# Subtracting two sets of low parts on POOL instead of VectorE in an encoder kernel

## The chip, the cores and the metric

The kernel runs on one core of one Trainium2 chip. The metric is the device time of one execution in microseconds (us); lower is better. The profiled times below come from one execution recorded by the hardware profiler. PE is the TensorE matrix engine, VectorE (DVE) does elementwise work, ACT is ScalarE, POOL is GpSimd, SP issues most DMAs.

## The reference, cut to what matters

One encoder layer with shared weights is applied to two groups of rows, a prompt of 256 and a sample of 1024, each row 1024 wide. The parts that matter here are the input projection and the expert layer:

```python
h = _rmsnorm(x, norm_mix[l])
(q_h, f_fw, f_bw, i_h, g_h, c_q, c_kv, k_pe, gl_h, gl_a) = jnp.split(h @ w_in[l], split_points, axis=-1)
y_h = _hgrn2_branch(...) @ w_br_h[l]
y_a = _mla_branch(...) @ w_br_a[l]
merged = jax.nn.sigmoid(gl_h) * y_h + jax.nn.sigmoid(gl_a) * y_a
x = x + merged @ w_out[l]
x = x + _peer(_rmsnorm(x, norm_ffn[l]), ...)

# _peer, for a block of 128 rows: 8 heads, 16 experts of 16384 for each
eidx, g = ...            # top 16 by product keys, softmax over their scores
u = jnp.take(u_tab, eidx, axis=0)
ve = jnp.take(v_tab, eidx, axis=0)
act = jax.nn.gelu(jnp.einsum('td,thkd->thk', zt, u), approximate=False) * g
return jnp.einsum('thk,thkd->td', act, ve)
```

All data are fp32.

## The kernel before

A product in fp32 precision is made from fp32r parts. `split` (L119 to L125) turns a tile into a high part, a cast on ACT (`nc.scalar.copy`, L123), and a low part, source minus high part, on VectorE (L124) or on an engine given as `eng`. `mm` then issues three matmuls: high by high (L140), high weight by low data (L141), low weight by high data (L142). With `whole` set, nothing is split and one plain fp32 matmul is issued (L138).

Two of the places that split weights are named by the change:

- The sample projection. `project` walks over 42 blocks of 128 columns of the input weights. `block` calls `load_w`: SP loads a `wraw` tile of 128x1024, ACT casts it to `wh`, and the low part becomes `wl`. Each block is multiplied with both halves of the 1024 sample rows, 48 matmuls a block. The prompt's projection runs the same code with `whole`, so it has no low part. `load_w` is also called for other weights (`wq`, `wo`, `wbh`, `wba`, `wuq`, `wk`, `wv`).
- The dense expert stage. 512 of the sample rows multiply with the whole expert tables. `first(b)`, for each of 128 blocks of 128 experts, loads `uraw` (128x1024) through `load_split`, splits it into `uh` and `ul`, multiplies it with the rows `zt` in 24 matmuls, applies gelu on ACT, multiplies by the gates (`ge`) on VectorE and splits the result into `ah` and `al`. `second(g)`, for each group of 4 blocks and each half of the 1024 output columns, loads and splits four `v` tiles (`vh`, `vl`, 128x512), issues 48 matmuls, and adds the results from PSUM into `acc` on VectorE (L1096).

The other rows, six groups of 128, go through gathered experts. POOL issues an indirect DMA for each of the 128 expert slots into a ring of 7 buffers of 128x1024. `u_steps` forms a dot product of each gathered `ug` with the row tile `zs` on VectorE (L938, L940). Then the `v` rows are gathered: `v_steps` weights and sums them on PE (L969, L976), while for two of the groups `v_slots` does it on VectorE, into `vacc` (L994, L996). These gathers run beside the sample projection, the attention and the dense expert stage until shortly before the end.

All queues are in order. The order in which instructions of independent parts are put on each engine's queue is set before the run by the framework's planner, which simulates a timeline with costs of its own; parts of the gathered path have higher priority there.

Of the kernel before, what the change touches and what calls it, by code (L numbers as in the profile page):

```python
# [24 lines left out]
P = 128  # L25
D = 1024
KD = D // P
# [23 lines left out]
def encoder(ctx, tc, I, O, dbg=None):  # L51
    nc = tc.nc
# [66 lines left out]
    def split(pool, src, shape, name, bufs=None, eng=None):  # L119
        kw = {} if bufs is None else {"bufs": bufs}  # L120
        hi = pool.tile(shape, F32R, name=name + "h", tag=name + "h", **kw)
        lo = pool.tile(shape, F32R, name=name + "l", tag=name + "l", **kw)
        nc.scalar.copy(hi, src)  # L123
        (eng or nc.vector).tensor_tensor(lo, src, hi.bitcast(F32), op=OP.subtract)  # L124
        return hi, lo  # L125

    def load_w(src, nk, cols, pool, whole=False, tag="w", bufs=3, nb=1, sp=None):
        raw = pool.tile([P, nk, cols], F32, name="wraw", tag=tag + "raw", bufs=bufs if tag == "w" else 1)  # L130
        cut = (lambda x: x.rearrange("p (b k) j -> p b k j", b=nb)) if nb > 1 else lambda x: x
        nc.sync.dma_start(cut(raw), src)
        x = (raw,) if whole else split(sp or pool, raw, [P, nk, cols], tag, bufs=2 if tag == "w" else 1)
        return [cut(a) for a in x]

    def mm(out, w, x, start, stop):
# [17 lines left out]
    def put(dst, src):  # L154

        if len(dst) == 1:
            nc.scalar.copy(dst[0], src)
        else:
            nc.scalar.copy(dst[0], src)
            nc.vector.tensor_tensor(dst[1], src, dst[0].bitcast(F32), op=OP.subtract)  # L160
# [43 lines left out]
    def project(s0, S, ap, wpool, bank, np_, whole):  # L204


        seg = min(S, 512)
        nseg = S // seg
        cps = seg // P
        H = parts(ap, [P, KD, S], "h", whole)  # L210
        ns = 256 if whole else 128
        for t0 in range(0, S, ns):
            xt = np_.tile([P, KD, ns], F32, name="xt", tag="xt", bufs=256 // ns)
            nc.sync.dma_start(xt, I["xT"][:, :, s0 + t0:s0 + t0 + ns])
            r = norm_T(np_, [xt[:, k] for k in range(KD)], KD, ns, "nA", bank, whole)
            for k in range(KD):
                hf = H[0][:, k, t0:t0 + ns] if whole else np_.tile([P, ns], F32, name="hf", tag="hf", bufs=3)
                nc.vector.scalar_tensor_tensor(out=hf, in0=xt[:, k], scalar=gains[:, G_MIX + k:G_MIX + k + 1],
                                               in1=r, op0=OP.mult, op1=OP.mult)
                if not whole:  # L220
                    put([a[:, k, t0:t0 + ns] for a in H], hf)
        yield

        def stage():
            return ap.tile([P, seg], F32, name="gt", tag="gt", bufs=3)

        def block(b, sink):
            w = load_w(I["wi"][b], KD, P, wpool, whole)
            for g in range(nseg):
                pm = bank()  # L230
                proj(pm[:, :seg], w, H, KD, g * seg, seg)
                sink(slice(s0 + g * seg, s0 + (g + 1) * seg), pm[:, :seg])

        def s_plain(dst, func=None):
            def f(ts_, pm):
                gt = stage()
                if func is None:
                    nc.scalar.copy(gt, pm)
                else:
                    nc.scalar.activation(out=gt, in_=pm, func=func)  # L240
                nc.scalar.dma_start(dst[:, ts_], gt)
            return f

        def s_silu(dst):
            def f(ts_, pm):
                gt = stage()
                nc.scalar.activation(out=gt, in_=pm, func=AF.Sigmoid)
                nc.vector.tensor_tensor(gt, pm, gt, op=OP.mult)
                nc.sync.dma_start(dst[:, ts_], gt)
            return f  # L250

        def s_forget(dst, c):
            def f(ts_, pm):
                gt = stage()
                nc.scalar.activation(out=gt, in_=pm, func=AF.Sigmoid)
                nc.scalar.activation(out=gt, in_=gt, func=AF.Identity, scale=omlb[:, c:c + 1], bias=lb[:, c:c + 1])
                nc.scalar.dma_start(dst[:, ts_], gt)
            return f

        def s_rows(dst):  # L260
            def f(ts_, pm):
                vT = stage()
                nc.scalar.copy(vT, pm)
                pt = bank()
                for c in range(cps):
                    nc.tensor.transpose(pt[:, c * P:(c + 1) * P], vT[:, c * P:(c + 1) * P], ident)
                gt = stage()
                nc.scalar.copy(gt, pt[:, :seg])
                nc.scalar.dma_start(dst[ts_].rearrange("(c p) j -> p c j", p=P), gt.rearrange("p (c j) -> p c j", j=P))
            return f  # L270

        for h in range(NH):
            block(B_FF + h, s_forget(fgd[1, h], h))
            block(B_FB + h, s_forget(fgd[0, h], NH + h))
            block(B_Q + h, s_silu(qhd[h]))
            block(B_I + h, s_rows(vhd[h]))
            block(B_G + h, s_silu(ghd[h]))
            yield
        for b in range(2):
            block(B_CKV + b, s_plain(lat[b]))  # L280
        block(B_PE, s_plain(lat[2]))
        for b in range(3):
            block(B_CQ + b, s_plain(lat[3 + b]))
        yield
        for b in range(8):
            block(B_GLH + b, s_plain(gated[b], AF.Sigmoid))
            block(B_GLA + b, s_plain(gated[8 + b], AF.Sigmoid))
        yield
# [766 lines left out]
            if t + 4 == TC:  # L1055
                nc.scalar.dma_start(gd[n * (P // TC) + c], gs[n, c].rearrange("p h t -> p (h t)"))

    def load_split(pool, src, shape, name, bufs):
        raw = pool.tile(shape, F32, name=name + "raw", tag=name + "raw", bufs=2)
        nc.sync.dma_start(raw, src)  # L1060
        return split(pool, raw, shape, name, bufs)

    def dense(routes, zt, acc, dp, up, bankS, bankV):

        nt = len(routes)
        nch = ND // TC
        held = {}
        a_of = {}

        def first(b):  # L1070
            u = load_split(up, I["uT"][b], [P, KD, P], "u", 2)
            if b % HB == 0:
                held["g"] = dp.tile([P, nch, HB, TC], F32, name="g", tag="g", bufs=2)
                nc.scalar.dma_start(held["g"].rearrange("p c h t -> p c (h t)"),
                                    gd[:, :, b * TC:(b + HB) * TC].rearrange("c p x -> p c x"))
            pm = bankS()
            for k in range(KD):
                mm(pm, [x[:, k] for x in u], [x[:, k] for x in zt], k == 0, k == KD - 1)
            ge = dp.tile([P, ND], F32, name="ge", tag="ge", bufs=2)
            nc.scalar.activation(out=ge, in_=pm, func=AF.Gelu)  # L1080
            gev = ge.rearrange("p (c t) -> p c t", t=TC)
            nc.vector.tensor_tensor(gev, gev, held["g"][:, :, b % HB], op=OP.mult)
            a_of[b] = (dp.tile([P, ND], F32R, name="ah", tag="ah", bufs=GE + 1),
                       dp.tile([P, ND], F32R, name="al", tag="al", bufs=GE + 1))
            put(a_of[b], ge)

        def second(g):
            for n in range(2):
                ns = slice(n * 512, (n + 1) * 512)
                vs = [load_split(dp, I["peer_v"][b * P:(b + 1) * P, ns], [P, 512], "v", 2 * GE)  # L1090
                      for b in range(g * GE, (g + 1) * GE)]
                for t in range(nt):
                    pm = bankV()
                    for i in range(GE):
                        mm(pm, [x[:, t * P:(t + 1) * P] for x in a_of[g * GE + i]], vs[i], i == 0, i == GE - 1)
                    nc.vector.tensor_tensor(acc[:, t, ns], pm, acc[:, t, ns], op=OP.add)  # L1096

        for t, r in enumerate(routes):
            nc.sync.dma_start(acc[:, t], x2d[r["tt"]:r["tt"] + P])
        first(0)  # L1100
        for g in range(P // GE):
            for b in range(g * GE + 1, (g + 1) * GE + 1):
                if b < P:
                    first(b)
            second(g)
        gfin = final_gain()
        for t, r in enumerate(routes):
            finish(acc[:, t], ring("sq"), r["tt"], gfin)
# [128 lines left out]
    up = ctx.enter_context(tc.tile_pool(name="DU", bufs=1, side="left"))  # L1237
# [78 lines left out]
```

## Time and profile before

| | |
|---|---|
| median of 3 runs | 4287.37 us (4286.51 to 4300.59) |
| profiled execution | 4300.6 us, span of the core 4298.8 us |
| busy PE / VectorE / ACT / POOL | 3802.2 / 3234.1 / 1559.9 / 1818.6 us |
| moved by DMA | 1263.92 MB, 294 GB/s on average |
| mean granted TensorE clock | 0.941 of full speed |

Busy times are sums over the whole span; an engine with a low share can still be full in one stage. A POOL instruction is mostly the issue of a gather, and its span in the profile is rough.

### The profile page before, as it was taken

The page shows a single profiled execution, that of the slowest core. Times are in us where ns is not written, and L with a number is a line of the kernel's source. Part 1 is how long each engine was busy: PE and PEld are TensorE (multiplying, and loading weights), DVE is VectorE, ACT ScalarE, POOL GpSimd, SP SyncE. Part 2 cuts the span into 40 slices and gives each one's busy share as a digit, 9 for nine tenths or more (in the row PEclk, how much of TensorE's full clock was granted, in tenths as well). Part 3 has the DMA queues.
Part 4 walks back from the last instruction along what each step waited for, and adds up shares of the span by engine and source line. Part 5 has one row for each costly group of instructions (what it writes and reads, how often), then busy time and mean ns, then how long its engine had stood idle before and what let it go on. Part 6 is the DMA issues. An engine that isn't in the chain of part 4 may idle for free.

```text
span 4298.8 us, 55005 instructions
## 1 busy us (share of the span) xinstructions
PE 3802.2 (88%) x18206; PEld 2734.5 (64%) x18206; DVE 3234.1 (75%) x8002; ACT 1559.9 (36%) x2600; POOL 1818.6 (42%) x1565
## 2 busy tenths in 40 slices
PE   6998999997777988877988489999999999899998
PEld 5777777775434753345644155677777877777786
DVE  4637988567988773986679985567668999999954
ACT  5555455454233214431201187522222222222232
POOL 0000644334444343774545512344446556666500
PEclk9999999998888999888999688999999999999999
DMA  5455899889999987998988847899999999999941
GB/s 160 123 183 152 324 344 343 315 305 319 318 311 313 323 312 272 328 339 326 334 293 285 292 181 292 325 322 339 334 333 356 339 358 362 365 364 346 326 140 64
DMA packets 508318, 1263.92 MB, mean 294 GB/s; under 512 B 49920, under 2 KB 203136, under 8 KB 505984
## 3 DMA queue, kind: packets, MB, share of 16 engines
q0 software_dynamic: 224352, 816.94, 52.9%
q1 hardware_dynamic: 197056, 354.05, 24.2%
q10 hardware_dynamic: 86624, 89.40, 6.1%
q8 instruction: 144, 2.36, 0.2%
q14 instruction: 142, 1.16, 0.1%
HBM read 1165.05 MB, written 95.16 MB: 293 GB/s over the span
## 4 chain that ended last, share of the span: by engine, by line
PE 55%; DMA 13%; DVE 12%; issue 12%; ACT 4%; POOL 2%; SPq 0%; another core or an unknown queue 0%; POOLq 0%; ACTq 0%; DVEq 0%
PE pm L140 12%; PE pm L141 11%; PE pm L142 11%; PE pm L138 7%; DMA vg<-peer_v,eit 5%; PE acc L976 5%; DVE ug L940 4%; DMA ug<-peer_u,ei 3%; PE pm L1053 3%; POOL ug L938 1%; PE pm L1034 1%; PE pm L437 1%; DVE vacc L996 1%; POOL vg L969 1%; PE pm L624 1%
## 5 line engine op out<-in xcount | busy, mean ns | idle before, releaser
L938 POOL DMA_INDIRECT ug<-peer_u,ei x768 | 908.9, 1184 | 800.8 <-DVE ug L940 334.2
L940 DVE SCALAR_TENSOR_TENSOR ug<-ug,zs 128x1024 f32<-128x1024 f32 x768 | 931.5, 1220 | 252.6 <-DMA ug<-peer_u,ei 189.3
L969 POOL DMA_INDIRECT vg<-peer_v,eit x512 | 540.7, 1056 | 752.8 <-DVE ug L940 308.9
L994 POOL DMA_INDIRECT vg<-peer_v,ei x256 | 354.7, 1385 | 207.0 <-DVE vacc L996 120.3
L141 PE MATMUL pm<-vl,ah 128*128 128x512 f32 x1024 | 405.1, 397 | 22.8 <-DVE vl L124 22.8
L140 PE MATMUL pm<-zth,uh 128*128 128x512 f32 x1024 | 406.3, 397 | 8.7 <-ACT ge L1080 6.0
L142 PE MATMUL pm<-zth,ul 128*128 128x512 f32 x1024 | 405.2, 396 | 0.0
L141 PE MATMUL pm<-ztl,uh 128*128 128x512 f32 x1024 | 404.8, 395 | 0.0
L976 PE MATMUL acc<-vg,zt 128*32 128x512 f32 x2048 | 284.6, 679 | 133.7 <-DMA vg<-peer_v,eit 132.8
L142 PE MATMUL pm<-vh,al 128*128 128x512 f32 x1024 | 400.6, 394 | 0.0
L140 PE MATMUL pm<-vh,ah 128*128 128x512 f32 x1024 | 374.9, 398 | 11.3 <-DVE acc L1096 5.5
L996 DVE SCALAR_TENSOR_TENSOR vacc<-vg,act,vacc 128x1024 f32<-128x1024 f32 x256 | 327.7, 1280 | 3.0 <-DMA vg<-peer_v,ei 0.9
L138 PE MATMUL pm<-xg,wraw 128*128 128x256 f32 (+1 forms) x1024 | 295.2, 441 | 4.1 <-DVE sr L855 4.1
L123 ACT CAST uh<-uraw 128x1024 fp32r<-128x1024 f32 x128 | 134.5, 1051 | 432.5 <-PE pm L141 413.2
L123 ACT CAST vh<-vraw 128x512 fp32r<-128x512 f32 x256 | 157.5, 618 | 352.0 <-DMA vraw<-peer_v 257.3
L140 PE MATMUL pm<-hh,wh 128*128 128x512 f32 x672 | 269.9, 402 | 5.0 <-ACT gt L240 3.0
L141 PE MATMUL pm<-hl,wh 128*128 128x512 f32 x672 | 268.3, 399 | 0.0
L142 PE MATMUL pm<-hh,wl 128*128 128x512 f32 x672 | 266.3, 396 | 0.0
L138 PEld LDWEIGHTS pm<-xg,wraw 128*128 128x128 f32 x1024 | 193.2, 194 | 80.6 <-issue 56.9
L141 PEld LDWEIGHTS pm<-vl,ah 128*128 128x128 f32 x1024 | 194.0, 189 | 75.1 <-DVE vl L124 31.5
L140 PEld LDWEIGHTS pm<-vh,ah 128*128 128x128 f32 x1024 | 194.1, 190 | 66.4 <-DVE acc L1096 14.1
L140 PEld LDWEIGHTS pm<-zth,uh 128*128 128x128 f32 x1024 | 192.2, 188 | 64.6 <-ACT ge L1080 11.4
(368 smaller groups left out, 7502.1 us busy)
## 6 DMA issues: line engine op xcount, KB each, us to landing
uraw<-uT SPq DMA_DIRECT2D x128, 512.0 KB
vraw<-peer_v SPq DMA_DIRECT2D x256, 256.0 KB
wraw<-wi SPq DMA_DIRECT2D x84, 512.0 KB
gd<-gs ACTq DMA_DIRECT2D x16, 2048.0 KB
g<-gd ACTq DMA_DIRECT2D x32, 1024.0 KB
wraw<-wq SPq DMA_DIRECT2D x48, 512.0 KB
wraw<-wo SPq DMA_DIRECT2D x24, 512.0 KB
ug<-peer_u,ei POOLq DMA_INDIRECT x768
```

The costliest lines, as they stand in the source:

```text
L123: nc.scalar.copy(hi, src)
L138: nc.tensor.matmul(out, w[0], x[0], start=start, stop=stop)
L140: nc.tensor.matmul(out, w[0], x[0], start=start, stop=False)
L141: nc.tensor.matmul(out, w[0], x[1], start=False, stop=False)
L142: nc.tensor.matmul(out, w[1], x[0], start=False, stop=stop)
L938: nc.gpsimd.indirect_dma_start(out=ug, out_offset=None, in_=I["peer_u"], in_offset=bass.IndirectOffsetOnAxis(ap=ei[:, s:s + 1], axis=0))
L940: nc.vector.scalar_tensor_tensor(out=ug, in0=ug, scalar=1.0, in1=zs, op0=OP.mult, op1=OP.mult, accum_out=dots[:, s:s + 1])
L969: nc.gpsimd.indirect_dma_start(out=vg, out_offset=None, in_=I["peer_v"], in_offset=bass.IndirectOffsetOnAxis(ap=eit[:, t:t + 1], axis=0))
L976: nc.tensor.matmul(acc[g_ * 32:(g_ + 1) * 32, n * 512:(n + 1) * 512], zt[:, h, g_, i], v_[:, n * 512:(n + 1) * 512], start=b == 0 and i == ...
L994: nc.gpsimd.indirect_dma_start(out=vg, out_offset=None, in_=I["peer_v"], in_offset=bass.IndirectOffsetOnAxis(ap=ei[:, s:s + 1], axis=0))
L996: nc.vector.scalar_tensor_tensor(out=acc, in0=vg, scalar=act[:, s:s + 1], in1=acc, op0=OP.mult, op1=OP.add)
L1053: nc.tensor.matmul(pm[:, j * P:(j + 1) * P], ol[:, j], oh[:, j], start=True, stop=True)
```

## The change

The low part of the sample projection's weight blocks and that of the expert blocks `u` are subtracted by POOL (`nc.gpsimd`) instead of VectorE. The casts, the loads and the matmuls stay. The low parts of all other tiles (`vl`, `al`, the other weights) stay on VectorE.

```diff
-    def load_w(src, nk, cols, pool, whole=False, tag="w", bufs=3, nb=1, sp=None):
+    def load_w(src, nk, cols, pool, whole=False, tag="w", bufs=3, nb=1, sp=None, eng=None):
...
-        x = (raw,) if whole else split(sp or pool, raw, [P, nk, cols], tag, bufs=2 if tag == "w" else 1)
+        x = (raw,) if whole else split(sp or pool, raw, [P, nk, cols], tag, bufs=2 if tag == "w" else 1, eng=eng)
...
         def block(b, sink):
-            w = load_w(I["wi"][b], KD, P, wpool, whole)
+            w = load_w(I["wi"][b], KD, P, wpool, whole, eng=nc.gpsimd)
...
-    def load_split(pool, src, shape, name, bufs):
+    def load_split(pool, src, shape, name, bufs, eng=None):
...
-        return split(pool, raw, shape, name, bufs)
+        return split(pool, raw, shape, name, bufs, eng)
...
         def first(b):
-            u = load_split(up, I["uT"][b], [P, KD, P], "u", 2)
+            u = load_split(up, I["uT"][b], [P, KD, P], "u", 2, nc.gpsimd)
```

## Rows read from the trace of the kernel before

**Rows 1.** The page's first part: busy us of each engine, share, instructions.
```profile
PE 3802.2 (88%) x18206; PEld 2734.5 (64%) x18206; DVE 3234.1 (75%) x8002; ACT 1559.9 (36%) x2600; POOL 1818.6 (42%) x1565
```

**Rows 2.** Busy time by stretch; behind POOL: clock, DMA share, GB/s.
```profile
430.00:570.00 140.00, 132.22 (x578) 107.64 (x577) 132.52 (x394) 54.53 (x75) 94.57 (x71) 0.98 0.91 332
570.00:710.00 140.00, 126.29 (x596) 103.96 (x595) 108.58 (x229) 87.20 (x124) 58.20 (x46) 0.95 0.93 330
710.00:850.00 140.00, 139.28 (x659) 109.47 (x658) 89.04 (x166) 62.53 (x91) 53.28 (x50) 1.00 0.92 330
850.00:1010.00 160.00, 152.24 (x768) 113.67 (x770) 108.94 (x272) 86.02 (x105) 69.08 (x66) 0.98 0.90 321
2740.00:3200.00 460.00, 456.17 (x2139) 339.30 (x2139) 295.48 (x457) 128.37 (x191) 210.80 (x191) 1.00 0.93 333
3200.00:3430.00 230.00, 230.00 (x1016) 182.39 (x1015) 200.08 (x267) 67.53 (x101) 132.09 (x102) 1.00 0.96 347
3430.00:3800.00 370.00, 337.38 (x1397) 264.34 (x1396) 354.28 (x499) 97.63 (x146) 233.18 (x183) 0.98 0.99 363
3800.00:4090.00 290.00, 282.31 (x1193) 222.86 (x1191) 275.65 (x314) 83.60 (x126) 173.91 (x120) 0.99 0.95 337
4090.00:4275.00 185.00, 184.51 (x801) 150.31 (x802) 89.25 (x127) 57.12 (x88) 0.37 (x1) 1.00 0.32 101
```

**Rows 3.** VectorE by line, 3430 to 4090 us: busy, mean ns, idle before.
```profile
L996 DVE SCALAR_TENSOR_TENSOR vacc<-vg,act,vacc 128x1024 f32<-128x1024 f32 x204 | 261.2, 1280 | 1.7
L940 DVE SCALAR_TENSOR_TENSOR ug<-ug,zs 128x1024 f32<-128x1024 f32 x102 | 123.3, 1220 | 1.7 <-DMA ug<-peer_u,ei 1.7
L124 DVE TENSOR_TENSOR vl<-vraw,vh 128x512 fp32r<-128x512 f32 x110 | 75.3, 685 | 1.6 <-ACT vh L123 1.6
L1096 DVE TENSOR_TENSOR acc<-pm,acc 128x512 f32<-128x512 f32 x109 | 71.6, 684 | 12.7 <-PE pm L142 12.4
L124 DVE TENSOR_TENSOR ul<-uraw,uh 128x1024 fp32r<-128x1024 f32 x54 | 65.9, 1220 | 10.8 <-ACT uh L123 10.7
L160 DVE TENSOR_TENSOR al<-ge,ah 128x512 fp32r<-128x512 f32 x52 | 34.9, 683 | 0.0
L1082 DVE TENSOR_TENSOR ge<-ge,g 128x512 f32<-128x512 f32 x52 | 34.5, 683 | 0.0
L940 DVE DVE_READ_ACCUMULATOR ug<-ug,zs 128x1 f32 x102 | 8.2, 80 | 0.0
```

**Rows 4.** PE by line, 3430 to 4090 us.
```profile
L141 PE MATMUL pm<-vl,ah 128*128 128x512 f32 x435 | 175.7, 404 | 22.8 <-DVE vl L124 22.8
...
L140 PE MATMUL pm<-zth,uh 128*128 128x512 f32 x428 | 170.2, 398 | 6.7 <-ACT ge L1080 6.0
...
L140 PE MATMUL pm<-vh,ah 128*128 128x512 f32 x432 | 149.7, 406 | 10.5 <-ACT vh L123 4.7 <-DVE acc L1096 4.6 <-issue 0.2
```

**Rows 5.** VectorE by line, 430 to 710 us.
```profile
L940 DVE SCALAR_TENSOR_TENSOR ug<-ug,zs 128x1024 f32<-128x1024 f32 x108 | 130.4, 1218 | 1.9 <-DMA ug<-peer_u,ei 1.9
L124 DVE TENSOR_TENSOR wl<-wraw,wh 128x1024 fp32r<-128x1024 f32 x20 | 24.4, 1220 | 5.8 <-ACT wh L123 5.7
```

**Rows 6.** POOL by line, whole span: what is not a DMA issue.
```profile
L1169 POOL MEMSET zt<- 128x1024 f32 x1 | 1.0, 952 | 437.4 <-PE pm L871 437.4
masks.py:199 POOL TENSOR_SCALAR_AFFINE_SELECT ident<-ident 128x128 f32<-128x128 f32 x1 | 0.3, 288 | 0.1
masks.py:197 POOL MEMSET ident<- 128x128 f32 x1 | 0.2, 206 | 0.3 <-POOLq L1307 0.3
...
L1307 POOL MEMSET const-float32-0.0<- 128x1 f32 x1 | 0.1, 100 | 0.2 <-issue 0.2
```

**Rows 7.** Timeline of ACT and VectorE about one `ul`: start us, duration us.
```profile
3916.28 1.05 ACT L123 CAST uh<-uraw 128x1024 fp32r<-128x1024 f32 x1 [0.25 <-PE pm L141]
...
3918.25 1.22 DVE L124 TENSOR_TENSOR ul<-uraw,uh 128x1024 fp32r<-128x1024 f32 x1
...
3925.59 1.06 ACT L123 CAST uh<-uraw 128x1024 fp32r<-128x1024 f32 x1 [6.06 <-PE pm L141]
```

## Prediction

> **What bounds the kernel now.** I read the page's busy line first [rows 1]: TensorE is the busiest engine at 88%, VectorE has 75%, POOL 42%. Those shares are averages over stages, so the second view is the table by stretches [rows 2], cut where the two edited steps lie. The sample projection (430 to 1010 us) runs with PE at 90 to 99% and VectorE falling from 95 to 64-68%. In the dense expert stage PE is full until 3430. From 3430 to 4090 VectorE is nearly full instead (354.28 + 275.65 = 629.9 of 660 us, 95%) and PE loses 32.6 + 7.7 = 40.3 us. Behind 4090 no gathers are left and PE is full again. So the stretch 3430 to 4090 is the one where VectorE's time is the kernel's time; what PE waits for there is mostly VectorE [rows 4]: 22.8 us for `vl`, 4.6 us for the accumulation into `acc`, and 6.0 us for `ge`, which itself waits on VectorE's `al`. The DMA engines are at 0.99 from 3430 to 3800, so they would be next in line.
>
> What VectorE does there is in [rows 3]. All of it except two groups (`acc`, whose other operand is a PSUM bank, 71.6 us, and the accumulator reads, 8.2 us) reads two tensors of SBUF: 86% of what is left once `ul` is gone.
>
> **What the change removes.** In the dense stage 128 subtractions `ul` leave VectorE, 54 of them in 3430 to 4090: 65.9 us there [rows 3]. In the sample projection 42 subtractions `wl` leave it (one per block of weight columns), 20 of them in 430 to 710: 24.4 us [rows 5]. The prompt's projection and the projections of `wq`, `wo` and the rest keep their code. No DMA is added or removed.
>
> **What it adds on POOL.** The trace has no POOL instruction with two tensor inputs, so its price is bounded [rows 6]. From below: a POOL memset of the same 128x1024 takes 0.95 us and reads nothing. From above: the one row that reads and writes is the select over 128x128, 288 ns against 100 ns for a one-column memset, so 1.47 ns a column, or 1.61 us for 1024; twice that, 3.2 us, is the upper end, as if the second operand cost a whole pass again. Between them I add one more stream at the memset's slope ((952 - 206) / 896 = 0.83 ns a column, 0.85 us) to the select's 1.61 us: 2.45 us, the value nearest to the row that does most of the same work. The Trainium skill (GPSIMD Engine Reference, Elementwise — side-by-side cycle accounting) gives 4497 ns for a two-input fp32 add of 2048 columns; an estimate from it is about 2.25 us here, and no row shows it. By that price the sum below would be some 10 us smaller.
>
> POOL has the room: 407.1 us busy of 660, plus 54 x 2.45 = 132 us, is 82%. A subtraction now stands in POOL's queue among the gathers, and it waits there for ACT's cast. What is queued behind it are gathers, and VectorE and PE wait for those. 303 gathers in 660 us [rows 2] is one every 2.2 us, and the ring has 7 buffers, so a queue held for 2 to 5 us is covered as long as the ring is full; without that cover each subtraction would cost up to its 2.45 us. The other side, `ul` being late for PE, I cost at nothing: the cast at 3916.28 gives an `ul` at 3919.5, and the next cast starts at 3925.59, when PE has left the block before [rows 7], so there are about 6 us of slack against 1.2 us more work and a gather in front.
>
> **What VectorE pays for a busy POOL.** This decides the sign. [Rows 2] show that the two engines are not independent: a POOL instruction (nearly all gathers) takes 53.28/50 = 1.07 and 69.08/66 = 1.05 us where VectorE is 64 and 68% busy, but 94.57/71 = 1.33 us and 173.91/120 = 1.45 us where it is 95% busy, with the DMA share about the same (0.92 and 0.90 against 0.91 and 0.95). So some of POOL's time is lost to VectorE's. Whether VectorE loses to POOL no row shows: its 1220 ns for `ug` is the same everywhere, but no POOL instruction there reads SBUF tensors. I bound the loss by nothing (they overlap freely) and by the whole hold: VectorE's two-input instructions stand still for as long as a POOL subtraction runs. I take the second: in the one direction that a row can show, POOL behind VectorE, the delay is there and grows with VectorE's share, and a POOL instruction that reads two tensors asks for more of what the two share than a gather does. The Trainium skill (SBUF — State Buffer, section SBUF: two separate sides) states such a rule: VectorE and GpSimd share a port pair that is locked for a whole instruction, against a VectorE instruction with two SBUF inputs if the GpSimd one reads SBUF. No row of before has such a pair of instructions; by it the sum is the one that follows, and by free overlap it is the first rival's.
>
> **The sum.** In 3430 to 4090, 54 holds of 2.45 us are 132.3 us. VectorE can use what is one-input work (79.8 of the 564.0 us left, 14%) or was idle anyway (30.1 of 660, 5%); 81% is lost, 107 us. Less the 65.9 us saved this is +41 us, and since the stretch has VectorE as its pace, the stretch grows by that. From 2740 to 3430 the same net, under 0.8 us for each of some 56 blocks, is 43 us against 690 - 495.6 = 194 us of VectorE idle time, and PE is full: nothing; if that cover were gone it would be 43 us. In 430 to 710, 20 x 2.45 x 0.81 = 39.7 less 24.4 is +15 us, with 38.9 us idle on VectorE: I take a third, +5. From 710 on VectorE is under 70%: nothing. Behind 4090 POOL is empty and VectorE half idle: nothing. Total +46 us. The profiled execution took 4300.6 us, the highest of the three; on its footing that is 4347. On the median of 4287.37, which I forecast, it is 4333.
>
> **The rivals.**
> *Free overlap (faster).* VectorE gets 65.9 us back in its full stretch. PE's waits for it there are 33.4 us; with the DMA at 0.99 until 3800 only the later part (7.7 us of PE idle time) is sure. So 8 to 33 us, and up to 10 us from the projection (PE is idle for 21.5 us in 430 to 710): about -25, 4262. For it: VectorE's durations don't move with POOL's gathers. Against it: POOL's do move with VectorE.
> *POOL is quick enough even with the hold (faster or same).* The hold costs nothing net when 54 x price x 0.81 is under 65.9, that is when a subtraction takes less than 1.51 us. At the memset's 0.95 us the stretch would lose 24 us: 4263. Against it: the select alone extrapolates to 1.61 us.
> *Nothing to be seen (same).* A milder loss, or a DMA-bound stretch 3430 to 3800, leaves the time within 20 us: 4287.
> *Late gathers (slower).* A subtraction that reaches the head of POOL's queue before its cast holds the gathers; if the planner, which orders every queue by costs of its own, puts it early, 170 subtractions at 0.3 us of exposed wait are +50 us, 4337. It decides once the ring of 7 runs empty, seen as VectorE idle before `ug` and `vacc` for DMA; now that is 1.7 us for `ug` in [rows 3].
>
> **How the numbers follow.** Hold: 0.43; free overlap: 0.23; quick POOL: 0.06; nothing: 0.20; late gathers: 0.08. The planner's new order can add or take some 15 us in any of them. About 0.5% (21 us) is what a measurement of this kernel can tell from no change. The hold passes +21 us in nine of ten, with late gathers that is 0.47 slower; free overlap and a quick POOL pass -21 us in three of four: 0.22 faster; 0.31 within. Range: at the price of 3.2 us the hold gives 54 x 3.2 x 0.81 - 65.9 = +74 in the dense stage and 20 x 3.2 x 0.81 - 24.4 = +27 at most in the projection, 4388 with both; I stop at 4380. Below, free overlap at its middle with half the planner's spread is 4254. The likeliest case alone is 4305 to 4375.
>
> **What would show it.** In the profile after: POOL rows for `ul` (128) and `wl` (42) with their price, 2.45 us or over; VectorE's mean for `vacc`, `ug`, `vl`, `al` and `ge` up from 1280, 1220, 685, 683 and 683 ns while `acc` stays at 684 (the hold), or unchanged (free overlap); PE idle time in the late dense stage up from 40 us or down towards 10; VectorE idle before `ug` for DMA grown (late gathers). The forecast is wrong if VectorE's two-input rows keep their means, or if POOL's price is under 1.5 us.

## Result, and the profile after

The changed kernel takes 4410.74 us (median of 4, 4406.5 to 4423.67) against 4286.94 us before (median of 4), a ratio of 1.0286 [1.0255, 1.0317]. The direction is that of the forecast, the size is not: +124 us where +46 were forecast, and 4410.74 lies above the range's upper end of 4380. The profiled execution of the changed kernel has a span of 4412.7 us, 114 us over the 4298.8 of before; what follows accounts for these 114.

The page's busy line of the changed kernel answers to [rows 1]:

```profile
PE 3841.9 (87%) x18206; PEld 2755.1 (62%) x18206; DVE 3361.1 (76%) x7832; ACT 1570.9 (36%) x2609; POOL 2210.7 (50%) x1735
```

VectorE lost exactly 170 instructions (8002 to 7832) and POOL gained them (1565 to 1735). Yet VectorE's busy time did not fall by 170 x 1.22 = 207 us; it rose by 127. VectorE by line, whole span, changed kernel (busy us, mean ns, idle before):

```profile
L940 DVE SCALAR_TENSOR_TENSOR ug<-ug,zs 128x1024 f32<-128x1024 f32 x768 | 1012.9, 1327 | 283.2 <-DMA ug<-peer_u,ei 207.7 <-issue 62.1 <-DMA vg<-peer_v,eit 9.2
L996 DVE SCALAR_TENSOR_TENSOR vacc<-vg,act,vacc 128x1024 f32<-128x1024 f32 x256 | 382.0, 1492 | 2.8
L124 DVE TENSOR_TENSOR vl<-vraw,vh 128x512 fp32r<-128x512 f32 x256 | 233.9, 917 | 64.5 <-ACT vh L123 62.2 <-issue 2.1
L1096 DVE TENSOR_TENSOR acc<-pm,acc 128x512 f32<-128x512 f32 x256 | 170.1, 683 | 53.8 <-PE pm L142 53.3
L1082 DVE TENSOR_TENSOR ge<-ge,g 128x512 f32<-128x512 f32 x128 | 138.1, 1086 | 51.1 <-ACT ge L1080 37.3 <-DMA g<-gd 12.0 <-ACT uh L123 1.2
L160 DVE TENSOR_TENSOR al<-ge,ah 128x512 fp32r<-128x512 f32 x128 | 97.9, 776 | 12.9 <-ACT ah L159 11.0 <-issue 0.7 <-PE pm L141 0.2
```

Against the means of [rows 3], every group with two SBUF operands is longer: `ug` 1220 to 1327 ns, `vacc` 1280 to 1492, `vl` 685 to 917, `ge` 683 to 1086, `al` 683 to 776. `acc`, whose other operand lies in PSUM, stays at 683. The new POOL rows of the same kernel, by line:

```profile
L124 POOL TENSOR_TENSOR ul<-uraw,uh 128x1024 fp32r<-128x1024 f32 x128 | 325.4, 2543 | 176.1 <-ACT uh L123 168.7 <-PE pm L142 5.1 <-issue 0.5
...
L124 POOL TENSOR_TENSOR wl<-wraw,wh 128x1024 fp32r<-128x1024 f32 x42 | 103.0, 2451 | 376.6 <-ACT wh L123 375.8
```

POOL ran its subtractions for 325.4 + 103.0 = 428 us. VectorE's time grew by 127 over a work load that is 207 smaller, so 334 us were lost, 78% of what POOL held. One such hold in the timeline of the changed kernel (start us, duration us; what it waited for in brackets):

```profile
3931.91 1.28 DVE L996 SCALAR_TENSOR_TENSOR vacc<-vg,act,vacc 128x1024 f32<-128x1024 f32 x1
...
3932.70 2.70 POOL L124 TENSOR_TENSOR ul<-uraw,uh 128x1024 fp32r<-128x1024 f32 x1
...
3933.11 2.83 DVE L124 TENSOR_TENSOR vl<-vraw,vh 128x512 fp32r<-128x512 f32 x1
...
3935.86 1.27 DVE L996 SCALAR_TENSOR_TENSOR vacc<-vg,act,vacc 128x1024 f32<-128x1024 f32 x1
...
3936.00 0.72 PE L141 MATMUL pm<-vl,ah 128*128 128x512 f32 x1 [3.03 <-DVE vl L124]
...
3936.94 0.63 PE L141 MATMUL pm<-vl,ah 128*128 128x512 f32 x1
```

The `vl` that began 0.4 us after POOL's subtraction took 2.83 us instead of 0.68 and ended half a microsecond after POOL did. PE waited 3.03 us for it. Then comes what the forecast had left out: the matmuls after the wait take 0.72 and 0.63 us instead of 0.39. The table by stretches (columns as in [rows 2]), cut around this wait, has the reason in the clock column, third from the end:

```profile
3920.00:3932.60 12.60, 12.60 (x57) 10.23 (x55) 12.49 (x13) 2.29 (x3) 10.91 (x8) 1.00 1.00 377
3932.60:3936.00 3.40, 0.37 (x3) 0.01 (x1) 3.40 (x3) 0.62 (x1) 3.24 (x3) 1.00 0.96 375
3936.00:3940.00 4.00, 4.00 (x11) 3.14 (x12) 2.99 (x3) 0.00 (x0) 3.20 (x3) 0.57 0.76 245
3940.00:3950.00 10.00, 9.40 (x40) 7.15 (x39) 9.59 (x13) 4.00 (x7) 3.86 (x4) 1.00 0.95 344
```

PE had been full at a granted clock of 1.00 (2.4 GHz), stood still for 3 us, and got 0.57 on average in the next 4 us, that is mostly 1.2 GHz, before it was back at 1.00. By an estimate from these two figures, a wait of 3 us cost PE another 4.0 x 0.43 = 1.7 us of its own time.

The two edited stages as wholes, first in the kernel before, then in the changed one:

```profile
438.00:1001.00 563.00, 540.02 (x2546) 427.45 (x2546) 424.70 (x1005) 280.72 (x378) 270.76 (x226) 0.98 0.92 332
...
2742.00:4267.00 1525.00, 1481.80 (x6500) 1152.29 (x6500) 1211.74 (x1656) 431.34 (x647) 749.47 (x593) 0.99 0.88 317
```

```profile
439.00:1033.00 594.00, 548.15 (x2527) 433.62 (x2526) 444.17 (x965) 294.19 (x386) 359.01 (x260) 0.96 0.89 309
...
2775.00:4382.00 1607.00, 1514.75 (x6518) 1168.98 (x6519) 1316.24 (x1536) 429.19 (x647) 1028.38 (x721) 0.97 0.86 301
```

The projection is 31 us longer and the dense stage 82; what lies between them is 1741 and 1742 us. In the dense stage PE's idle time (length less busy) goes from 43 to 92 us, +49, and its busy time, for the same matmuls, from 1481.8 to 1514.8, +33: the clock. In the projection it is +23 idle and +8 busy. VectorE, counted as above, lost 261 of POOL's 325 us in the dense stage (80%) and 71 of 103 in the projection (69%).

To see where the time went, both traces are cut at the same work: where PE begins block 20 of the projection (701.2 us before, 730.9 in the changed kernel), block 60 of the experts (3427.5 and 3491.7) and block 116, behind which no gathers are left (4126 and 4240). Before, then changed:

```profile
438.00:701.20 263.20, 244.63 (x1107) 200.49 (x1107) 226.60 (x572) 131.47 (x180) 148.14 (x113) 0.96 0.95 345
701.20:1001.00 299.80, 295.38 (x1440) 226.96 (x1440) 198.10 (x434) 149.25 (x199) 122.62 (x113) 0.99 0.90 321
2742.00:3427.50 685.50, 682.77 (x3135) 518.97 (x3136) 494.06 (x721) 192.49 (x288) 340.90 (x290) 1.00 0.94 338
3427.50:4126.00 698.50, 658.03 (x2755) 518.60 (x2754) 654.06 (x848) 197.42 (x299) 408.57 (x304) 0.99 0.94 341
4126.00:4267.00 141.00, 141.00 (x613) 114.73 (x612) 63.62 (x87) 41.43 (x62) 0.00 (x0) 1.00 0.30 94
```

```profile
439.00:730.90 291.90, 257.82 (x1139) 209.00 (x1138) 244.71 (x571) 152.01 (x202) 182.57 (x127) 0.94 0.91 310
730.90:1033.00 302.10, 290.33 (x1390) 224.62 (x1389) 199.46 (x395) 142.18 (x184) 176.44 (x133) 0.98 0.88 309
2774.80:3491.70 716.90, 697.38 (x3175) 524.67 (x3176) 530.13 (x665) 191.93 (x290) 469.72 (x347) 1.00 0.92 323
3491.70:4240.00 748.30, 675.88 (x2731) 529.32 (x2730) 714.10 (x794) 195.94 (x297) 532.25 (x364) 0.95 0.91 321
4240.00:4382.00 142.00, 141.67 (x615) 115.17 (x614) 72.01 (x78) 41.32 (x62) 26.41 (x11) 1.00 0.29 93
```

In the projection the first 20 blocks take 28.7 us more and the other 22 take 2.3. Of the experts, blocks 0 to 59 take 31.4 us more, blocks 60 to 115 take 49.8, and the rest 1.0. In blocks 60 to 115 VectorE is 95% busy (94% before), and its own busy time grew by 60 us. What PE waits for, in the dense stage and then in the projection of the changed kernel (us in total, times, longest):

```profile
PE pm L141 <- DVE vl L124: 49.2, 21, 5.5
PE pm L140 <- DVE acc L1096: 18.8, 17, 3.5
...
PE pm L142 <- POOL ul L124: 1.6, 2, 1.1
```

```profile
PE pm L140 <- DVE gt L248: 18.1, 7, 4.6
```

In the dense stage PE waits for VectorE, as in [rows 4], only longer. For POOL's `ul` itself it waits 1.6 us. In the projection it waits for the gate eviction `gt` (L248: VectorE multiplies the PSUM tile by its sigmoid), for which PE of before lost 0.4 us.

### The profile page after: what moved, and what is told of

Read it like the earlier page. It is cut to its first block, busy times and chain, and to the rows that moved or that the text cites. A ratio compares the mean times of both kernels' runs of the same rounds, so it can differ in the third digit from the quotient of the medians.

```text
span 4412.7 us, 55052 instructions
## 1 busy us (share of the span) xinstructions
PE 3841.9 (87%) x18206; PEld 2755.1 (62%) x18206; DVE 3361.1 (76%) x7832; ACT 1570.9 (36%) x2609; POOL 2210.7 (50%) x1735
## 4 chain that ended last, share of the span: by engine, by line
PE 30%; issue 11%; DVE 10%; DMA 9%; POOL 6%; ACT 2%; SPq 0%; POOLq 0%; another core or an unknown queue 0%; DVEq 0%; ACTq 0%
PE pm L141 6%; PE pm L140 6%; PE pm L142 6%; DMA ug<-peer_u,ei 4%; PE pm L138 4%; DVE ug L940 3%; PE acc L976 3%; DMA vg<-peer_v,eit 3%; PE pm L1053 3%; POOL ug L938 2%; DVE vacc L996 2%; POOL vg L994 1%; PE pm L1034 1%; POOL ul L124 1%; POOL vg L969 1%
## 5 line engine op out<-in xcount | busy, mean ns | idle before, releaser
L940 DVE SCALAR_TENSOR_TENSOR ug<-ug,zs 128x1024 f32<-128x1024 f32 x768 | 1012.9, 1327 | 283.2 <-DMA ug<-peer_u,ei 207.7
L141 PE MATMUL pm<-vl,ah 128*128 128x512 f32 x1024 | 415.1, 407 | 49.2 <-DVE vl L124 49.2
L124 POOL TENSOR_TENSOR ul<-uraw,uh 128x1024 fp32r<-128x1024 f32 x128 | 325.4, 2543 | 176.1 <-ACT uh L123 168.7
L996 DVE SCALAR_TENSOR_TENSOR vacc<-vg,act,vacc 128x1024 f32<-128x1024 f32 x256 | 382.0, 1492 | 2.8
L994 POOL DMA_INDIRECT vg<-peer_v,ei x256 | 311.5, 1217 | 134.8 <-DVE vacc L996 61.5
L124 POOL TENSOR_TENSOR wl<-wraw,wh 128x1024 fp32r<-128x1024 f32 x42 | 103.0, 2451 | 376.6 <-ACT wh L123 375.8
L140 PE MATMUL pm<-hh,wh 128*128 128x512 f32 x672 | 271.8, 405 | 20.3 <-DVE gt L248 18.1
L124 DVE TENSOR_TENSOR vl<-vraw,vh 128x512 fp32r<-128x512 f32 x256 | 233.9, 917 | 64.5 <-ACT vh L123 62.2
```

The costliest lines, as they stand in the source:

```text
L140: nc.tensor.matmul(out, w[0], x[0], start=start, stop=False)
L141: nc.tensor.matmul(out, w[0], x[1], start=False, stop=False)
L940: nc.vector.scalar_tensor_tensor(out=ug, in0=ug, scalar=1.0, in1=zs, op0=OP.mult, op1=OP.mult, accum_out=dots[:, s:s + 1])
L994: nc.gpsimd.indirect_dma_start(out=vg, out_offset=None, in_=I["peer_v"], in_offset=bass.IndirectOffsetOnAxis(ap=ei[:, s:s + 1], axis=0))
L996: nc.vector.scalar_tensor_tensor(out=acc, in0=vg, scalar=act[:, s:s + 1], in1=acc, op0=OP.mult, op1=OP.add)
```

## The experiments

Two theories stood against each other. *Hold*: while a POOL instruction reads SBUF, VectorE's instructions with two SBUF operands stand still. *Queue*: POOL's queue is longer, so gathers come later and low parts are late. A gain by free overlap was already excluded by the result. Ratios are to the kernel before on the same chip, whose median was 4271.94 to 4293.49 us from call to call; lengths of the dense stage and of the projection are read as above (1525 and 563 us before). Where the diff says so, a kernel starts from the changed one, otherwise from the one before.

### Each half alone

`u` alone and `w` alone, from the changed kernel:

```diff
 # u only
-            w = load_w(I["wi"][b], KD, P, wpool, whole, eng=nc.gpsimd)
+            w = load_w(I["wi"][b], KD, P, wpool, whole)
```

> Only the 128 subtractions ul are on POOL; wl is back on VectorE. Theory (hold, and PE's clock behind it): in the trace of the change the dense stage grew by 82 us (first zth matmul to the last, 1517 to 1599 us), by PE idle time and a lower granted clock; so some +80 us, 4367, and the sample projection as before. Rival (the planner's new order did it, wherever it put things): the parts don't add up to the whole, this one can land anywhere between 4287 and 4411.

```diff
 # w only
-            u = load_split(up, I["uT"][b], [P, KD, P], "u", 2, nc.gpsimd)
+            u = load_split(up, I["uT"][b], [P, KD, P], "u", 2)
```

> Only the 42 subtractions wl are on POOL. Theory: the projection grew by 33 us and nothing gave it back, so about 4320, with the whole of the change close to the sum of this and the other part. My prediction's term for it was +5 (4292). Rival (planner): no sum.

Measured: `u` alone 1.0189 [1.0165, 1.0212], dense stage 1599 us (+74), projection 560. `w` alone 1.0113 [1.0095, 1.0132], projection 599 us (+36), dense stage 1523. Both halves cost, each in its own stage, and 1.9% and 1.1% add up to 3.0%, against 2.9% for the whole, as the theory expected and the planner's rival did not. Traces with an unchanged dense stage have it at 1519 to 1525 us, and those with an unchanged projection have that at 560 to 566, so a stage length from one trace is good to a few us; the part between the stages, the same code in all, takes 1704 to 1750. The half of the projection, forecast at +5 us, is a third of the loss.

### The hold made without the move

VectorE keeps `ul`; POOL does an additional instruction on the raw tile, which nothing but SP's next load of that buffer waits for. Once it reads two tensors, once it only writes, for about the same time:

```diff
-        return split(pool, raw, shape, name, bufs)
+        x = split(pool, raw, shape, name, bufs)
+        if name == "u":
+            nc.gpsimd.tensor_tensor(raw, raw, x[0].bitcast(F32), op=OP.subtract)
+        return x
```

> In both memset kernels so far an engine stood in its own queue for POOL (VectorE's ul 120 us, ACT's one-column read 456 us), so they could not tell. Here POOL works on the uraw buffer once its readers are done: this kernel subtracts uh from it in place (two SBUF inputs, about 2.45 us). Only the next load into that buffer waits for POOL, as in the change. VectorE keeps its own ul. Theory (hold): VectorE's two-input rows get longer by 200 us or more in all, acc stays at 684 ns; +130 to +170 us over the kernel before. Rival (POOL's queue): as the next kernel.

```diff
+            for n in (KD, KD, 5):
+                nc.gpsimd.memset(raw[:, 0:n], 0.0)
```

> The same with memsets of about 2.5 us in all on the uraw buffer. POOL is as busy and gathers stand behind it as long, but it reads nothing. Theory (hold): VectorE's rows keep their means and the time is within 20 us of before. Rival (POOL's queue makes the gathers late): +50 us or more, VectorE idle before ug and vacc for DMA.

Measured: with two reads 1.0307 [1.027, 1.0344], dense stage 1654 us (+129); without reads 1.0075 [1.0052, 1.0099], 1558 us (+33). By line, first with two reads, then without:

```profile
L996 DVE SCALAR_TENSOR_TENSOR vacc<-vg,act,vacc 128x1024 f32<-128x1024 f32 x256 | 400.1, 1563 | 1.1
L124 DVE TENSOR_TENSOR vl<-vraw,vh 128x512 fp32r<-128x512 f32 x256 | 227.9, 900 | 37.5 <-ACT vh L123 34.0 <-issue 3.4
L1099 DVE TENSOR_TENSOR acc<-pm,acc 128x512 f32<-128x512 f32 x256 | 170.0, 682 | 32.6 <-PE pm L142 31.5 <-issue 0.7
...
L1063 POOL TENSOR_TENSOR uraw<-uraw,uh 128x1024 f32<-128x1024 f32 x128 | 335.4, 2620 | 123.5 <-DVE ul L124 108.0 <-DVE fint L182 9.5 <-issue 2.3
```

```profile
L996 DVE SCALAR_TENSOR_TENSOR vacc<-vg,act,vacc 128x1024 f32<-128x1024 f32 x256 | 328.0, 1281 | 13.3 <-DMA vg<-peer_v,ei 10.4 <-DVE acc L1100 0.6
L124 DVE TENSOR_TENSOR vl<-vraw,vh 128x512 fp32r<-128x512 f32 x256 | 173.6, 687 | 61.3 <-ACT vh L123 60.7 <-issue 0.4
...
L1064 POOL MEMSET uraw<- 128x1024 f32 (+1 forms) x384 | 327.9, 857 | 192.7 <-DVE ul L124 183.8
```

POOL is occupied for 335 and 328 us, the same. With reads `vacc` and `vl` grow to 1563 and 900 ns; without, they keep 1281 and 687. `acc` does not move. That is the hold, shown apart from the move, and the pair differs by 96 us of dense stage. With reads the time is at the lower end of what was expected (+131 us by the ratio); without, the expected 20 us were exceeded, and the remaining +33 did not fit the hold, which had nothing to say there. Its waits showed SP's queue held by the raw buffer (`uraw` free only after POOL) and the `v` loads late behind it:

```profile
SPq L1060 <- POOL uraw L1064: 666.4, 119, 13.0
...
PE pm L140 <- ACT vh L123: 21.2, 7, 4.6
```

So the same again with a third raw buffer for `u`, and the `u`-only kernel with a third one beside it:

```diff
-        raw = pool.tile(shape, F32, name=name + "raw", tag=name + "raw", bufs=2)
+        raw = pool.tile(shape, F32, name=name + "raw", tag=name + "raw", bufs=3 if name == "u" else 2)
```

> POOL's memsets on the uraw buffer (no read) with three uraw buffers. The dense stage was 1558 us with two. Theory (its 33 us are loads that came late because the buffer was released late): 1525 to 1537. Rival (gathers behind the memsets in POOL's queue): 1558 again.

> ul alone on POOL with three uraw buffers instead of two, so that the next load doesn't wait for POOL. The dense stage was 1599 us with two, 1525 before. If the late release costs what the memset kernel shows (33 us), the stage falls to about 1566 to 1580; if the hold is all of it, it stays at 1590 to 1600.

Measured: no reads, three buffers 1.0000 [0.9977, 1.0024], dense stage 1522 us; `u` alone, three buffers 1.0181 [1.0142, 1.022], 1599 us as with two. Writing for 2.57 us on POOL 128 times, among the gathers, costs nothing. That rules out the queue theory for the dense stage: POOL's time is free there, its reads are not. And a third buffer gives `u` alone nothing back, so the late release of the raw buffer is no part of its loss. The kernel with two reads was not run with a third buffer; how much of its +129 the late release makes up stays open.

### Which blocks pay

`u` on POOL for the first 42 of 128 blocks, and for the other 86, with `w` on VectorE:

```diff
-            u = load_split(up, I["uT"][b], [P, KD, P], "u", 2, nc.gpsimd)
+            u = load_split(up, I["uT"][b], [P, KD, P], "u", 2, nc.gpsimd if b < 42 else None)
```

> POOL subtracts ul for the first 42 of 128 blocks only, which are those up to the point where VectorE becomes full; wl stays on VectorE. My prediction put nothing there, as VectorE had 194 us idle. Theory now: the same order of nothing, at most +12 us (PE idle grew by 9 us there and the clock dipped from 1.00 to 0.99 over 525 us). Rival (what VectorE loses early is only moved to the full rounds): 42 x 0.65 us, +27.

> POOL subtracts ul for blocks 42 to 127 only. Prediction: +41 us. Theory now: +60 to +70 us, 41 us of PE idle time and the rest by PE's clock, which falls behind each stall. The two halves add up to the kernel with all of ul on POOL (+75). Rival (planner): no sum.

Measured: early blocks 1.0017 [0.9995, 1.0039], late blocks 1.0121 [1.0083, 1.0159]. Their dense stages, early then late:

```profile
2703.00:4243.00 1540.00, 1489.90 (x6516) 1160.02 (x6516) 1228.52 (x1620) 428.82 (x648) 823.61 (x635) 0.99 0.88 315
```

```profile
2717.00:4297.00 1580.00, 1500.44 (x6502) 1162.12 (x6503) 1291.54 (x1572) 430.85 (x648) 946.30 (x679) 0.98 0.87 306
```

+15 and +55 us, against +74 for all. The time of the whole kernel does not tell the early blocks from no change, but the stage does. Their +15 is just over the 12 expected and well under the rival's 27, and the late +55 just under the 60 expected. The late blocks pay 36 us of PE idle time (79.6 against 43.2) and 19 of PE busy time; the early ones 7 and 8.

The same for `w`, the 20 blocks of columns below `B_CQ`, and the 22 from there on, with `u` on VectorE:

```diff
-            w = load_w(I["wi"][b], KD, P, wpool, whole, eng=nc.gpsimd)
+            w = load_w(I["wi"][b], KD, P, wpool, whole, eng=nc.gpsimd if b < B_CQ else None)
```

> wl on POOL for the first 20 of the 42 blocks of the sample projection (the forget, query, input and gate columns, where VectorE is 95 to 78% busy and evicts the gates itself). Theory: the whole of what wl on POOL cost the projection (563 to 599 us) is here: about +30 us. Rival (each of the 42 costs the same): +17.

> wl on POOL for the last 22 blocks, where VectorE is 64 to 68% busy and ACT alone evicts. Theory: within 6 us of the projection's 563 us. Rival (each costs the same): +19 us.

Measured: first 20 1.0069 [1.0047, 1.0091], projection 588 us (+25); last 22 1.0025 [1.0002, 1.0047], 575 us (+12). The first come nearer to the theory than to the rival. They have the wait for the gate eviction; the last 22 have none of it and still pay, against the expectation of at most 6. Of their 12 us, 3.5 had come about before block 20, where that kernel is as before; in the changed kernel itself the last 22 blocks take only 2.3 us more.

```profile
PE pm L140 <- DVE gt L248: 17.5, 6, 5.2
```

### Does the hold cost where VectorE has room?

If the price is VectorE's lack of room, it should go when VectorE has less to do in the dense stage. `v_slots` was given up, for one and then for both of the two groups, so that PE sums their `v` rows:

```diff
-    for r in r1:
-        r["acc"] = vp
+    r1[0]["acc"] = vp
```

> The kernel before, with the second expert products of one of the last two gathered groups summed on PE instead of VectorE (v_steps in place of v_slots): 128 vacc instructions (164 us) leave VectorE, and 512 short matmuls (some 31 us by the share in the earlier rounds, 3.85 us for 32) come to PE. If VectorE's time is the kernel's time from 3430 to 4090 us, its 40 us of PE idle time and 10 us of low clock go, less the 31 us: about -15 us. Rival (that stretch is bound by DMA at 0.99): no gain, +31.

> The same for both groups: 328 us leave VectorE, 62 us come to PE. VectorE is no longer full anywhere in the dense stage. 62 less 50: about +10 us, 4285; rival (DMA): +50 or more.

Measured: 1.013 [1.009, 1.0169] and 1.0198 [1.0163, 1.0233]. Both expectations missed. They counted about half of PE's new work: the second kernel puts 1024 more matmuls on PE (7539 - 6500 in the records), 1593 - 1482 = 111 us of PE time. The first has a second reason: from 3300 to 3800 us VectorE is still 93% busy with the `vacc` of the one group left, and PE is idle for 32.7 us there, as before (32.6). With both groups on PE its idle time in the stage falls from 43 to 9 us. Then both, `v` on PE and `u` on POOL:

> ul on POOL in the kernel whose last two gathered groups are summed on PE (dense stage 1602 us there, VectorE 58% busy, PE idle 9 us). Theory (the hold costs where VectorE is full): VectorE has the room, the stage stays within 20 us of 1602. Rival (a fixed price of a POOL subtraction, wherever it stands): +74 us as with ul alone on POOL.

Measured: 1.0229 [1.0193, 1.0264]. Dense stages, `v` on PE without and with the move of `u`:

```profile
2730.00:4332.00 1602.00, 1593.07 (x7539) 1172.55 (x7538) 930.15 (x1439) 434.67 (x647) 656.08 (x596) 1.00 0.85 303
```

```profile
2732.00:4357.00 1625.00, 1600.39 (x7543) 1172.94 (x7541) 998.79 (x1315) 430.94 (x647) 938.26 (x722) 1.00 0.85 299
```

With VectorE at 58% and 61% the move costs 23 us (+16 idle, +7 busy) instead of 74: 3 more than the theory allowed, and far from the rival. Instructions are held all the same: `ge` takes 1337 ns and `ug` of the whole span 1323, and VectorE's time grows by 69 us although 156 left it. So the hold is there with VectorE at 61% too, but costs less. That this is due to VectorE's room is argued and not shown apart: PE has 111 us more work in these two kernels. Neither kernel is a better one, since PE is the bound of both.

### Four controls that mixed two things

Additional POOL work was first put elsewhere. On `ul` before VectorE writes it, two reads (`uraw` less `uraw`), then memsets of two and five eighths of the tile:

```diff
+        if extra:
+            extra(lo, src)
         nc.scalar.copy(hi, src)
...
+    def extra(lo, src):
+        nc.gpsimd.tensor_tensor(lo, src, src, op=OP.subtract)
```

> VectorE makes every ul itself, as before; ahead of it POOL writes the same buffer with uraw minus uraw, a POOL subtraction with two SBUF inputs (2.45 us) that nothing needs. Theory (hold): VectorE loses about 238 us in the dense stage as in the change, but keeps the 154 us of its own subtractions, so more than the change's dense part: +150 to +240 us, 4440 to 4525, with vacc, ug, vl, ge rows longer and acc at 684 ns. Rival (POOL's queue is full and the gathers come late): as the change's dense part, +80, 4367, and VectorE's rows at their old means.

> As the kernel with two reads, but POOL fills the same buffer with memsets of zeros of about the same total time (2 x 0.95 us and a part of 640 columns, some 2.5 us), which read nothing. VectorE then writes the true ul. Theory (hold): POOL is as busy and the gathers wait as long, but VectorE's rows keep their means (1280, 1220, 685, 684 ns), so within 20 us of before, 4287 to 4305. Rival (POOL's queue): as long as with two reads.

And into a scratch tile after the split, two reads and then memsets, with a one-column copy on ACT that waits for it:

```diff
+            if b:
+                nc.scalar.copy(dp.tile([P, 1], F32, name="tiny", tag="tiny", bufs=1), held["scr"][:, 0, 0:1])
+            scr = held["scr"] = dp.tile([P, KD, P], F32, name="scr", tag="scr", bufs=1)
+            nc.gpsimd.tensor_tensor(scr, last["u"], u[0].bitcast(F32), op=OP.subtract)
```

> VectorE makes every ul as before. POOL makes the same subtraction (uraw minus uh, 2.45 us) once more into a scratch buffer that no VectorE and no PE instruction waits for; a one-column read by ACT ties its pace to the dense blocks. Theory (hold): VectorE loses in the dense stage what it lost in the change (about 238 us) without the 156 us that the change saved it; the kernel with a POOL subtraction of 2.03 us ahead of ul lost 167 us in VectorE's rows for 93 us, so this one some +130 us over the kernel before. Rival (POOL's queue): as the next kernel.

> The same with memsets of about 2.5 us in all into the scratch buffer, which read nothing. In the first memset kernel VectorE's ul waited 120 us in VectorE's queue for POOL's memsets; here nothing waits for POOL but the gathers. Theory (hold): VectorE's rows at their old means and the time within 20 us of before. Rival (POOL's queue, late gathers): +65 us as with the first memset kernel, and VectorE idle before ug and vacc for DMA.

Measured: on `ul` 1.0216 [1.0182, 1.0249] with reads and 1.015 [1.0131, 1.0168] without; scratch 1.0397 [1.0362, 1.0432] and 1.0167 [1.0131, 1.0203]. In both kernels without reads VectorE's means are those of before, as the hold says, but the time is not, and both expectations of no change missed. With reads the means are longer (`vacc` 1517 ns in scratch), but those expectations missed in time as well: on `ul` +92 us where +150 to +240 were expected, in scratch +170 where +130 were. By line and by waits, memsets on `ul` and then memsets in scratch:

```profile
L126 DVE TENSOR_TENSOR ul<-uraw,uh 128x1024 fp32r<-128x1024 f32 x128 | 156.5, 1223 | 120.8 <-POOL ul L1064 120.5
```

```profile
ACT tiny L1073 <- POOL scr L1076: 456.5, 126, 8.4
```

In the first VectorE stood in its queue for POOL (120.5 us), in the second ACT did (456.5 us). The times of these four don't tell the theories apart; their instruction means do.

### One operand read instead of two

Two copies of `uh` into the raw tile, 2 x 1.35 us:

```diff
+            for n in (KD, KD):
+                nc.gpsimd.tensor_copy(raw[:, 0:n], x[0].bitcast(F32)[:, 0:n])
```

> As the kernels that work on the uraw buffer, with two POOL copies of uh into it (one SBUF input each) in place of the subtraction or the memsets. Two reads made the dense stage 1654 us, no read 1558, before 1525. If the hold needs only that POOL reads SBUF at all, VectorE's rows lengthen by the copies' time and the stage lands near 1654 for the same POOL time; if it needs both inputs, near 1558 with VectorE's rows unchanged.

Measured: 1.0438 [1.0402, 1.0474], dense stage 1735 us. VectorE and POOL by line:

```profile
L996 DVE SCALAR_TENSOR_TENSOR vacc<-vg,act,vacc 128x1024 f32<-128x1024 f32 x256 | 359.4, 1404 | 1.8
...
L1064 POOL COPY uraw<-uh 128x1024 f32<-128x1024 f32 x256 | 344.1, 1350 | 246.2 <-DVE ul L124 244.6 <-issue 0.6
```

`vacc` at 1404 ns shows that a POOL instruction with a single SBUF input holds VectorE too. The time is not the hold's alone: PE waited 72.3 us for ACT's cast of `ah` and 66.2 for that of `uh`, and the raw buffer was released late with only two of them. How much belongs to what stays open.

## Why the forecast had the sign and missed the size

**POOL's price.** Forecast 2.45 us from bounds of 0.95 and 3.2; measured 2451 ns (`wl`) and 2543 (`ul`) on average. Right.

**The hold, 81% of it lost.** Right in kind, and in size for the dense stage, where it was worked out: 80% there, 69% in the projection. `acc` is untouched, as the row of [rows 3] with a PSUM operand let expect. The hold is shown by the pair of reads against writes. The Trainium skill (SBUF — State Buffer, section SBUF: two separate sides) says that the shared port pair goes for a whole instruction to whichever starts first, against a VectorE instruction with two SBUF inputs only if the GpSimd one reads SBUF; the runs agree, with a `vl` of 2.83 us instead of 0.68 and with memsets that leave it at 0.687.

**3430 to 4090, +41 us.** Right in mechanism and nearly in size: the same work, blocks 60 to 115, takes 49.8 us more. VectorE's busy time grew by 60.0 us there and its idle time fell by 10.2, so VectorE still sets the pace. The missing 9 us go with POOL's price: 56 subtractions fall into these blocks, at 2.67 us each instead of 2.45, and the forecast's own sum with these figures gives 56 x (2.67 x 0.81 - 1.22) = 53. Counted on PE, the same 49.8 us are 31.9 of idle time and 17.9 of matmuls at a lower clock. These are two counts of one stretch of time and don't add up; no run shows what a PE at full clock would have saved there.

**2740 to 3430, nothing.** This step failed: *"43 us against 690 - 495.6 = 194 us of VectorE idle time, and PE is full: nothing"*. Blocks 0 to 59 take 31.4 us more. The 194 us were an average over two unlike parts. Cut at block 44, about where `vacc` begins, the kernel before and then the changed one:

```profile
2742.00:3267.00 525.00, 522.27 (x2442) 388.96 (x2443) 345.12 (x537) 148.11 (x222) 242.40 (x216) 1.00 0.93 333
3267.00:3427.50 160.50, 160.50 (x695) 130.00 (x694) 148.94 (x185) 44.38 (x67) 98.50 (x75) 1.00 0.96 353
```

```profile
2774.80:3318.40 543.60, 530.63 (x2463) 391.84 (x2464) 357.80 (x487) 146.16 (x221) 336.82 (x257) 0.99 0.91 320
3318.40:3491.70 173.30, 166.75 (x713) 132.84 (x712) 172.34 (x179) 45.77 (x70) 132.91 (x91) 1.00 0.94 330
```

Behind block 44 VectorE was 93% busy already; with the hold it is at 99% and sets the pace, for 12.8 us more. The other 18.6 us came in blocks 0 to 43, with VectorE at 66% and PE nearly full: 10 of them are PE's idle time in a few single waits (3.8 us for `ah`, 2.8 for `al`), and 8 its slower busy time. Idle time on average does not cover a hold that stands in front of what PE needs next. With POOL on the first 42 blocks alone the stage grew by 15.

**430 to 710, +5, and nothing from 710 on.** The first of these failed too: *"with 38.9 us idle on VectorE: I take a third, +5"*. It took 28.7 us; with these 20 blocks alone on POOL the whole projection grew by 25. PE waits there for evictions in VectorE's in-order queue: `gt` reads PSUM and is not held itself (684 ns on average, 686 before), yet it stands behind instructions that are, and PE's wait for it in the projection went from 0.4 to 18.1 us. PE at a lower clock added 8 in the whole projection. The second was right within 2.3 us in the changed kernel; with the last 22 blocks alone on POOL the projection grew by 12, and no single wait explains it.

**Late `ul`, late gathers, planner.** The first at nothing: right, 1.6 us. The rival of late gathers fell: VectorE's wait for gathered `u` in the dense stage went from 72.6 to 81.5 us, and in the kernel of writes alone POOL's time cost nothing. For the projection no such kernel was run. Against the planner stands that the two halves add up, and the early and late blocks nearly (15 + 55 of 74).

**Sum.** Forecast 41 + 0 + 5 = 46; measured 49.8 + 31.4 + 28.7 in these three stretches, 2.3 and 1.0 in the two others that were put at nothing, together 113, and 1 between the stages. Of the 67 us that were missing, 55 lie in the two terms for which VectorE's average idle time had been taken as cover, and 9 in the full stretch. On PE's own count the 113 are 49 + 23 = 72 of idle time and 33 + 8 = 41 of slower busy time. The rivals of free overlap and of a quick POOL are out by the first two points.

## What to carry to other kernels

Before elementwise work is moved from VectorE to POOL, ask whether POOL's instruction reads SBUF and whether what VectorE runs meanwhile has two SBUF operands. Where both hold, as here, 1.22 us saved was paid with 2.5 us of holding, of which 80% was lost in the dense stage. Idle time of an in-order engine is not cover as an average: cut the stretch where its work changes, and ask whether the idle time lies in front of the instruction that the busiest engine waits for. One engine's waits and slower work, and another engine's growth, can be two counts of the same time, so take one of them. A control that adds work on an engine must not make another engine's queue wait for it: compare the means of instructions first, then the times.

## What was not expected

After a PE wait of 3 us the granted clock fell from 1.00 to 0.57 over the next 4 us; with hardly a wait left in the dense stage (`v` on PE, 9 us idle) it was 1.00 on average over the stage. A POOL subtraction of a tile from itself took 2.03 us on average, that of two different tiles 2.43 to 2.71 from kernel to kernel. A POOL copy with one input took 1.35 us and held VectorE too (`vacc` 1404 ns), while 2.57 us of POOL memsets a block left every VectorE mean as it was and cost no time at all.
